# The input projection of layer A, one product at a time over all of k, with 512-column matmuls over both parts of x

## The chip, the cores and the metric

The kernel runs on one core of a Trainium2 chip. The metric is the device time of one execution in microseconds (us); the median of three runs is given, and one further execution was taken with the hardware profiler. TensorE (PE in the profile) multiplies, with PEld for its weight loads; VectorE (DVE), ScalarE (ACT) and GpSimd (POOL) work on tiles in the on-chip memory SBUF, and DVE and ACT also read PE's accumulators in PSUM; SyncE (SP) issues nearly all DMA transfers.

## The reference

Two layers of a small encoder over 512 tokens, width 2048, all in float32. The change is in the first step of layer A, the matrix product `h @ w_in` with its 2048 x 8192 weight:

```python
def pool_mixer_layer(x, norm_g, w_in, w_group, scale, w_out):
    h = rmsnorm(x, norm_g)
    proj = h @ w_in
    u, gate = proj[..., :W_A], proj[..., W_A:]
...
    pooled = jnp.stack(
        [causal_mean_pool(u[:, :, gi], w) - u[:, :, gi] for gi, w in enumerate(POOL_WINDOWS)],
        axis=2)
    y = jnp.einsum('bsgc,gcd->bsgd', pooled, w_group).reshape(B, S, W_A) * scale
    y = y * jax.nn.silu(gate)
    return x + y @ w_out
```

## The kernel before, in words

**Three matmuls for one product.** A float32 product is made of three passes: every operand is split into a rounded high part (dtype fp32r, a copy on ACT) and the rest, the low part (a subtraction on DVE), and PE adds w_hi x_hi, w_hi x_lo and w_lo x_hi in a PSUM accumulator. `split` (L145 to L147) does this for one operand: L146 is the copy on ACT, L147 the subtraction on DVE.

**Seven products for eight.** The projection has 64 blocks of 128 output columns. Four of them (32 to 35) are done in the plain way while x is read in (lines around L372 to L374 of the kernel before). The other 60 are done as 30 pairs. A pair is a 2 x 2 block product: two output blocks by two halves of the tokens (H = 256 tokens each), over the 2048 rows of k, which are taken two tiles of 128 at a time; the eight such steps are called j (NJ = 8). The block product is made with seven products in place of eight, in the manner of Strassen and Winograd: each of the seven multiplies a sum of weight blocks with a sum of x blocks. The seven sums of x are made once (`x_parts`, `x_sums`) and stay in SBUF as `xh[j]` and `xl[j]`, seven slices of 256 columns each. The sums of the weights are made for each pair.

**The loop over pairs (L397 on).** For each pair there are four rounds q of two j. `w_combos` loads the weights of a round (two DMAs of 256 KB, L299, on SP's queue), makes the sums (L302 on DVE, L304 and L305 on POOL), and splits all seven slices at once: L308 on ACT, L309 on DVE, 128 x 1792 each. `seven` then issues, for each of the two j and each of the seven products, the three matmuls L325, L327 and L329, each of 256 columns, 42 in a round and 168 in a pair. The seven products accumulate in seven halves of four PSUM banks (k0 to k3, two sets of them). After the last j `gather` adds the halves into the two outputs (L335 on ACT, L336 to L339 on DVE), and two DMAs (L348) store them in DRAM. For the first eight output blocks `pool_tile` (L241 to L257, on DVE) pools them before they are stored. In the first pairs `square` (L390 to L395) and `norm_r` make the row norms of x beside the loop.

**What sets the order.** Each engine works through its own instructions in the order of the program; a scheduler lays the instructions of all engines out at build time. A tile pool hands out a fixed number of buffers per tag (`bufs`): the write into a reused buffer waits until the last reader of its old content is done. In the loop the tag `raw` has three buffers of 8 KB per partition, `hi` and `lo` two each. SP's queue holds the loads of weights, the stores of outputs and the reads of x, in one order.

**Behind the loop** (L412 on) the stage of the grouped product and the output projection begins: `pooled_tile` reads the first eight pooled blocks back (L424) and `proj` multiplies them with `awg` by three 512-column matmuls for each weight tile (L141 to L143).

## Time and profile before

| what | value |
|---|---|
| median of three runs | 1954.69 us (1954.32 to 1954.99) |
| the profiled execution: its own time | 1954.67 us |
| its span in the profile | 1952.5 us |
| granted TensorE clock, mean over the span | 0.999 |
| PE busy, share of the span | 1920.2 us, 98% |
| DVE, ACT, POOL busy | 1275.8, 820.5, 264.8 us |
| DMA | 235.52 MB, mean 121 GB/s |
| the chain that ended last: PE's share | 91% |

A row of the profile's groups gives line, engine, operation, output and inputs with their shapes, how often, then busy time, mean ns of one, and the idle time of the engine just before with what ended it. A row of the timeline gives the start in us from the span's start, the duration in us, engine, line, operation, how many are merged, and in brackets the idle time before it and what released it. A row of the windows gives a stretch, its length, the busy time of each engine with the number of its instructions, then the granted clock, the busy share of the DMA engines and GB/s. Matmuls overlap in PE's pipeline, so that a matmul's duration is longer than the distance to the next; what PE can do in a time is read from the distances.

### The profile page before, as it was taken

The numbers are of one execution on the slowest core, as the hardware profiler recorded it, in microseconds if no ns is written. First come the engines' busy times: TensorE is split into PE (matmuls) and PEld (weight loads), VectorE is DVE, ScalarE is ACT, GpSimd is POOL, SyncE is SP. The second block draws the span as 40 slices with busy tenths as digits, with TensorE's granted clock in tenths as the row PEclk, the third lists the DMA queues.
The fourth block names the chain that finished last, engine by engine and source line by source line (L and its number), as shares of the span: only waits on it lengthen the run. The fifth ranks groups of instructions, "written<-read, shape, count | busy, mean of one in ns | idle before, by whom it ended". The sixth has DMA issues, their size and how long they took to land.

```text
span 1952.5 us, 30593 instructions
## 1 busy us (share of the span) xinstructions
PE 1920.2 (98%) x11356; PEld 1708.7 (88%) x11356; DVE 1275.8 (65%) x2289; ACT 820.5 (42%) x1561; POOL 264.8 (14%) x404
## 2 busy tenths in 40 slices
PE   8999999999999999999999999999999999999999
PEld 7899999999999878888888888888888888888887
DVE  8766676797666587486695567473344788797432
ACT  7533333333333443333333454332244777785221
POOL 0442323344322100000000000000010111110000
PEclk9999999999999999999999999999999999999999
DMA  6644344335444465334344343333322111121632
GB/s 199 202 135 140 119 138 133 125 125 173 136 124 131 154 212 159 113 121 143 114 130 130 119 146 124 92 92 97 98 92 76 56 39 53 45 70 48 218 119 87
DMA packets 168133, 235.52 MB, mean 121 GB/s; under 512 B 14896, under 2 KB 95152, under 8 KB 167984
## 3 DMA queue, kind: packets, MB, share of 16 engines
q1 hardware_dynamic: 167696, 233.37, 38.0%
q8 instruction: 89, 1.46, 0.3%
q14 instruction: 60, 0.49, 0.1%
q10 hardware_dynamic: 288, 0.20, 0.0%
HBM read 208.35 MB, written 25.17 MB: 120 GB/s over the span
## 4 chain that ended last, share of the span: by engine, by line
PE 91%; DVE 4%; ACT 2%; DMA 1%; issue 1%; SPq 0%; DVEq 0%; ACTq 0%
PE mm L143 16%; PE mm L141 16%; PE mm L142 16%; PE k L329 9%; PE k L325 9%; PE k L327 9%; PE sc L731 2%; PE mm L605 2%; PE mm L607 1%; PE mm L606 1%; PE mm L625 1%; DVE lo L309 1%; PE mm L626 1%; DMA raw<-awin 1%; PE mm L627 1%
## 5 line engine op out<-in xcount | busy, mean ns | idle before, releaser
L123 ACT CAST whi<-raw 128x512 fp32r<-128x512 f32 (+2 forms) x421 | 253.1, 609 | 521.2 <-PE mm L142 451.5
L325 PE MATMUL k<-xh,hi 128*128 128x256 f32 x1680 | 460.0, 283 | 0.0
L327 PE MATMUL k<-xl,hi 128*128 128x256 f32 x1680 | 460.0, 283 | 0.0
L124 DVE TENSOR_TENSOR wlo<-raw,whi 128x512 fp32r<-128x512 f32 (+2 forms) x421 | 281.4, 672 | 231.0 <-ACT whi L123 228.9
L329 PE MATMUL k<-xh,lo 128*128 128x256 f32 x1680 | 418.1, 284 | 4.3 <-DVE lo L309 4.1
L308 ACT CAST hi<-raw 128x1792 fp32r<-128x1792 f32 x120 | 202.8, 1690 | 373.4 <-PE k L329 264.9
L309 DVE TENSOR_TENSOR lo<-raw,hi 128x1792 fp32r<-128x1792 f32 x120 | 248.5, 2071 | 155.7 <-ACT hi L308 155.4
L143 PE MATMUL mm<-bt,wlo 128*128 128x512 f32 x860 | 335.3, 390 | 0.2 <-DVE wlo L124 0.2
L141 PE MATMUL mm<-bt,whi 128*128 128x512 f32 x860 | 334.8, 389 | 0.0
L142 PE MATMUL mm<-bt,whi 128*128 128x512 f32 x860 | 334.5, 389 | 0.0
L327 PEld LDWEIGHTS k<-xl,hi 128*128 128x128 f32 x1680 | 322.5, 192 | 0.0
L325 PEld LDWEIGHTS k<-xh,hi 128*128 128x128 f32 x1680 | 322.5, 192 | 0.0
L329 PEld LDWEIGHTS k<-xh,lo 128*128 128x128 f32 x1680 | 296.7, 192 | 6.0 <-DVE lo L309 5.5
L141 PE MATMUL mm<-at,whi 128*128 128x512 f32 x516 | 201.2, 391 | 3.3 <-ACT whi L123 3.3
L143 PE MATMUL mm<-at,wlo 128*128 128x512 f32 x516 | 202.1, 392 | 1.7 <-DVE wlo L124 1.7
L142 PE MATMUL mm<-at,whi 128*128 128x512 f32 x516 | 202.1, 392 | 0.0
L143 PEld LDWEIGHTS mm<-bt,wlo 128*128 128x128 f32 x860 | 161.4, 188 | 34.6 <-DVE wlo L124 0.6
L141 PEld LDWEIGHTS mm<-bt,whi 128*128 128x128 f32 x860 | 161.4, 188 | 33.7 <-ACT whi L123 0.2
L142 PEld LDWEIGHTS mm<-bt,whi 128*128 128x128 f32 x860 | 161.4, 188 | 33.5
L304 POOL TENSOR_TENSOR raw<-raw 128x256 f32<-128x256 f32 x120 | 102.6, 855 | 430.0 <-DVE raw L302 406.4
L143 PEld LDWEIGHTS mm<-at,wlo 128*128 128x128 f32 x516 | 97.3, 188 | 23.6 <-DVE wlo L124 3.4
L141 PEld LDWEIGHTS mm<-at,whi 128*128 128x128 f32 x516 | 97.1, 188 | 23.6 <-ACT whi L123 3.9
(1174 smaller groups left out, 2584.7 us busy)
## 6 DMA issues: line engine op xcount, KB each, us to landing
raw<-awin SPq DMA_DIRECT2D x240, 256.0 KB, 3.3
raw<-awo SPq DMA_DIRECT2D x128, 256.0 KB, 2.8
raw<-bwin SPq DMA_DIRECT2D x80, 256.0 KB, 2.7
raw<-awg SPq DMA_DIRECT2D x64, 256.0 KB, 2.8
raw<-bwo SPq DMA_DIRECT2D x59, 256.0 KB, 2.8
scr<-e SPq DMA_DIRECT2D x56, 256.0 KB, 2.6
raw<-wkvb SPq DMA_DIRECT2D x32, 256.0 KB, 3.0
raw<-wqb SPq DMA_DIRECT2D x32, 192.0 KB, 2.4
```

The lines of the kernel that those rows point to most:

```text
L123: A.copy(hi[:, :n], raw[:, :n])
L124: V.tensor_tensor(lo[:, :n], raw[:, :n], f(hi[:, :n]), ALU.subtract)
L141: T.matmul(dst, wh, xh, start=first, stop=False)
L142: T.matmul(dst, wh, xl, start=False, stop=False)
L143: T.matmul(dst, wl, xh, start=False, stop=last)
L304: G.tensor_tensor(c[:, :, 6, :], c[:, :, 4, :], c[:, :, 2, :], ALU.add)
L308: A.copy(hi, c[:, :, 1:8, :])
L309: V.tensor_tensor(lo, c[:, :, 1:8, :], f(hi), ALU.subtract)
L325: T.matmul(dst, hi[:, j % 2, wi, :], xh[j][:, xi, :], start=first, stop=False, skip_group_check=True)
L327: T.matmul(dst, hi[:, j % 2, wi, :], xl[j][:, xi, :], start=False, stop=False, skip_group_check=True)
L329: T.matmul(dst, lo[:, j % 2, wi, :], xh[j][:, xi, :], start=False, stop=last, skip_group_check=True)
L605: T.matmul(acc, ch[:, tsl], hi, start=(k == 0), stop=False)
```

## The change

The seven products of a pair are now made one after the other, each over all eight j (`in_pair`, which takes the place of `w_combos`, `banks`, `seven` and `gather`). The numbers p1 to p7 below are the order of the `product` calls.

- The high and low part of x lie side by side (`xx`), so that w_hi x_hi and w_hi x_lo are one matmul of 512 columns (L314) into the two halves of a PSUM bank; w_lo x_hi stays a matmul of 256 columns (L316) into the first half. A product is 8 x 2 matmuls, a pair 112 in place of 168.
- The weights of a pair come as two DMAs of 1 MB (L300, tiles m1 and m2), and a sum or a split covers 128 x 1024 (all j) at a time: two sums on DVE (s1 = a21 + a22 at L325; a21 + a11 at L334), two on POOL (s2 = s1 + a11 at L329; s2 + a12 at L338), seven splits (L146 and L147). `hi` and `lo` have three buffers of one product each; `raw` keeps its three buffers of 1 MB, and a pair holds two of them.
- Three banks per pair. ACT reads banks out between products (L324, L327, L331, L333, L336, L343), as the same bank takes up the next product; DVE adds the pieces (L328, L337, L340, L341, L344, L345). `put` stores the outputs, as before.
- The pool behind `pool_tile` and `square` has three buffers in place of six, and the squares one accumulator in place of two.

```diff
-            h = xcp.tile([P, 7, H], F32R, tag="xh", name="xh")
-            lo = xcp.tile([P, 7, H], F32R, tag="xl", name="xl")
-            xh[j], xl[j] = h, lo
+            xx[j] = xcp.tile([P, 7, 2, H], F32R, tag="xx", name="xx")
+            h, lo = xh[j], xl[j] = xx[j][:, :, 0, :], xx[j][:, :, 1, :]
...
+        def in_pair(pair):
+            m1, m2 = (w7.tile([P, NJ, 2, P], F32, tag="raw", name="raw", bufs=3) for _ in range(2))
+            for m, t in enumerate((m1, m2)):
+                nc.sync.dma_start(t.rearrange("p j k n -> p (j k n)"), awin[2 * pair + m])
+            a11, a12, a21, a22 = m1[:, :, 0, :], m1[:, :, 1, :], m2[:, :, 0, :], m2[:, :, 1, :]
+            s1, s2 = (w7.tile([P, NJ, P], F32, tag=t, name=t, bufs=1) for t in ("s1", "s2"))
+            bx, bb, bc = (ps7.tile([P, 2, H], F32, tag=f"k{i}", name=f"k{i}") for i in range(3))
+            def part(a):
+                hi = w7.tile([P, NJ, P], F32R, tag="hi", name="hi", bufs=3)
+                lo = w7.tile([P, NJ, P], F32R, tag="lo", name="lo", bufs=3)
+                split(a, hi, lo)
+                return hi, lo
+            def product(w, xi, b, first, last):
+                hi, lo = w
+                for j in range(NJ):
+                    T.matmul(b, hi[:, j, :], xx[j][:, xi, :, :], start=first and j == 0, stop=False,
+                             skip_group_check=True)
+                    T.matmul(b[:, 0, :], lo[:, j, :], xh[j][:, xi, :], start=False, stop=last and j == NJ - 1,
+                             skip_group_check=True)
...
+            product(part(a11), 2, bx, True, False)
+            A.copy(p1, bx)
+            V.tensor_tensor(s1, a21, a22, ALU.add)
+            product(part(s1), 4, bc, True, False)
+            A.copy(s5, bc)
+            V.tensor_tensor(p1[:, 0, :], p1[:, 0, :], p1[:, 1, :], ALU.add)
+            G.tensor_tensor(s2, s1, a11, ALU.add)
+            product(part(s2), 5, bb, True, False)
+            A.copy(z[:, 0], bb)
+            product(part(a12), 0, bx, False, True)
+            A.copy(p1[:, 1, :], bx[:, 1, :])
+            V.tensor_tensor(a21, a21, a11, ALU.add)
+            product(part(a21), 3, bb, False, False)
+            A.copy(z[:, 2], bb)
+            V.tensor_tensor(e[:, 0, :], p1[:, 1, :], bx[:, 0, :], ALU.add)
+            G.tensor_tensor(s2, s2, a12, ALU.add)
+            product(part(s2), 1, bc, False, True)
+            V.tensor_tensor(z[:, 0], z[:, 0], bc, ALU.add)
+            V.tensor_tensor(z[:, 2], z[:, 2], s5, ALU.add)
+            product(part(a22), 6, bb, False, True)
+            A.copy(z[:, 1], bb)
+            V.tensor_tensor(e[:, 1:4, :], z[:, :, 0, :], z[:, :, 1, :], ALU.add)
+            V.tensor_tensor(e[:, 1:4, :], e[:, 1:4, :], p1[:, 0:1, :].broadcast_to([P, 3, H]), ALU.add)
...
-        tp[0] = c1.enter_context(tc.tile_pool(name="tpool1", bufs=6, **tile_))
+        tp[0] = c1.enter_context(tc.tile_pool(name="tpool1", bufs=3, **tile_))
```

The order of the instructions on each engine is fixed when the kernel is built. On DVE, in the middle of the loop, one pair took these rows before: four rounds of a split (lo) and of a sum for a round to come (raw), with the four additions of the pair that had just ended in between. A number behind a tile's name tells its buffer's content apart; in brackets stands what the instruction waits for.

```order
L309 TENSOR_TENSOR lo_3268<-raw_3261,hi_3267 128x1792 [waits PE_49,Activation_49]
L302 TENSOR_TENSOR raw_3379<-raw_3379 128x2x256 [waits DMAHW3_49,DMAHW2_49]
L309 TENSOR_TENSOR lo_3320<-raw_3313,hi_3319 128x1792 [waits PE_49,Activation_49]
L302 TENSOR_TENSOR raw_3431<-raw_3431 128x2x256 [waits DMAHW7_49,DMAHW6_49,DVE_49]
L309 TENSOR_TENSOR lo_3386<-raw_3379,hi_3385 128x1792 [waits PE_49,Activation_49]
L302 TENSOR_TENSOR raw_3483<-raw_3483 128x2x256 [waits DMAHW1_49,DMAHW0_49,DVE_49]
L309 TENSOR_TENSOR lo_3438<-raw_3431,hi_3437 128x1792 [waits PE_49,Activation_49]
L302 TENSOR_TENSOR raw_3535<-raw_3535 128x2x256 [waits DMAHW3_49,DMAHW2_49]
L336 TENSOR_TENSOR e_3365<-e_3365,k0_3153 128x512 [waits Activation_49]
```

In the changed kernel DVE has these rows at the end of one pair (raw_3123 and raw_3124 are its m1 and m2) and the start of the next (raw_3312 and raw_3313): lo_3248 and lo_3270 are the low parts of p6 and p7 of the pair, lo_3326, lo_3348 and lo_3371 those of p1, p2 and p3 of the next.

```order
L147 TENSOR_TENSOR lo_3248<-s2_3128,hi_3247 128x1024 [waits PE_49,Activation_49]
L325 TENSOR_TENSOR s1_3316<-raw_3313 128x1024 [waits DMAHW1_49]
L334 TENSOR_TENSOR raw_3313<-raw_3313,raw_3312 128x8x128 [waits DMAHW6_49,DVE_49]
L147 TENSOR_TENSOR lo_3270<-raw_3124,hi_3269 128x1024 [waits PE_49,Activation_49]
L337 TENSOR_TENSOR e_3135<-p1_3134,k0_3129 128x256 [waits DMAHW4_49,DMAHW3_49,Activation_49]
L147 TENSOR_TENSOR lo_3326<-raw_3312,hi_3325 128x1024 [waits PE_49,Activation_49]
L341 TENSOR_TENSOR z_3132<-z_3132,s5_3133 128x512 [waits Activation_49]
L340 TENSOR_TENSOR z_3132<-z_3132,k2_3131 128x512 [waits PE_49]
L147 TENSOR_TENSOR lo_3348<-s1_3316,hi_3347 128x1024 [waits Activation_49]
L147 TENSOR_TENSOR lo_3371<-s2_3317,hi_3370 128x1024 [waits PE_49,Activation_49]
L344 TENSOR_TENSOR e_3135<-z_3132 128x768 [waits DVE_49,Activation_49]
L345 TENSOR_TENSOR e_3135<-e_3135,p1_3134 128x768 [waits DVE_49]
```

The sums of the next pair (L325, L334), which wait for its m2, stand in the queue ahead of the low part of p7 of the pair in hand. On SP's queue a pair had eight loads of 256 KB before, each waiting for the DVE alone that frees its buffer, and two stores.

```order
L299 DMA raw_3261<-awin 128x2x256 [waits DMAHW7_49,DMAHW6_49,DVE_49]
L299 DMA raw_3261<-awin 128x2x256
L299 DMA raw_3313<-awin 128x2x256 [waits DMAHW1_49,DMAHW0_49,DVE_49]
L299 DMA raw_3313<-awin 128x2x256
L299 DMA raw_3379<-awin 128x2x256 [waits DMAHW4_49,DMAHW5_49,DMAHW2_49,DVE_49]
L299 DMA raw_3379<-awin 128x2x256 [waits DMAHW3_49]
L348 DMA scr_3149<-e_3143 256x1x256 [waits DVE_49,Activation_49]
L348 DMA scr_3151<-e_3143 128x512
```

In the changed kernel a pair has two loads of 1 MB; m2 (raw_3313 here) goes into the buffer of m1 of the pair in hand (raw_3123) and so waits for DVE and POOL, the last readers of that m1.

```order
L300 DMA raw_3312<-awin 128x2048 [waits DMAHW1_49,DVE_49]
L358 DMA scr_3119<-e_2962 128x512 [waits DMAHW7_49,DVE_49]
L358 DMA scr_3121<-e_2962 128x512 [waits DMAHW0_49]
L300 DMA raw_3313<-awin 128x2048 [waits DMAHW2_49,DVE_49,Pool_49]
L300 DMA raw_3501<-awin 128x2048 [waits DMAHW5_49,DVE_49]
```

The load of m2 for the next pair moved behind the store of the pair that has ended and behind POOL's second sum of the pair in hand.

More of the change, by code (lines that the diff above doesn't have):

```diff
@@ L312, in banks @@
-        def banks():
-            return [ps7.tile([P, 2, H], F32, tag=f"k{i}", name=f"k{i}") for i in range(4)]
-        SEVEN = ((2, 0, 0, 0), (0, 6, 1, 0), (1, 2, 2, 0), (3, 4, 3, 0),
-                 (5, 5, 0, 1), (6, 1, 1, 1), (4, 3, 2, 1))
-        def seven(ks, w, j):
-            hi, lo = w
-            for wi, xi, b, h in SEVEN:
-                dst = ks[b][:, h, :]
-                first, last = j == 0 and h == 0, j == NJ - 1
-                T.matmul(dst, hi[:, j % 2, wi, :], xh[j][:, xi, :], start=first, stop=False,
-                         skip_group_check=True)
-                T.matmul(dst, hi[:, j % 2, wi, :], xl[j][:, xi, :], start=False, stop=False,
-                         skip_group_check=True)
-                T.matmul(dst, lo[:, j % 2, wi, :], xh[j][:, xi, :], start=False, stop=last,
-                         skip_group_check=True)
@@ L341, in gather, with put @@
+        def put(e, pair):
+            for i in range(2):
+                v = e[:, 2 * i:2 * i + 2, :]
                 o = 2 * pair + i
```

59 lines of the change are left out of this document (17 added, 42 removed).

## The prediction

> **What bounds the kernel now.** I read the page first: busy time and the chain that ended last.
>
> ```profile
> PE 1920.2 (98%) x11356; PEld 1708.7 (88%) x11356; DVE 1275.8 (65%) x2289; ACT 820.5 (42%) x1561; POOL 264.8 (14%) x404
> ...
> PE 91%; DVE 4%; ACT 2%; DMA 1%; issue 1%; SPq 0%; DVEq 0%; ACTq 0%
> ```
>
> PE is the bound over the whole span. Next the timeline of PE: first the distances between matmuls in the loop over pairs (340), in a later stage (1400) and in the stretch that mixes both widths (17 to 19), then the two ends of the loop.
>
> ```profile
> 17.73 0.28 PE L372 MATMUL k<-h,hi 128*128 128x256 f32 x1
> ...
> 18.09 0.39 PE L372 MATMUL k<-xh,hi 128*128 128x512 f32 x1
> ...
> 18.78 0.28 PE L373 MATMUL k<-xl,hi 128*128 128x256 f32 x1
> ...
> 55.05 0.28 PE L325 MATMUL k<-xh,hi 128*128 128x256 f32 x1
> ...
> 340.39 0.28 PE L325 MATMUL k<-xh,hi 128*128 128x256 f32 x1
> ...
> 341.11 0.28 PE L325 MATMUL k<-xh,hi 128*128 128x256 f32 x1
> ...
> 666.43 0.28 PE L329 MATMUL k<-xh,lo 128*128 128x256 f32 x1
> 669.25 0.50 PE L141 MATMUL mm<-at,whi 128*128 128x512 f32 x1 [2.54 <-ACT whi L123]
> ...
> 1400.16 0.39 PE L143 MATMUL mm<-bt,wlo 128*128 128x512 f32 x1
> ...
> 1409.68 0.39 PE L143 MATMUL mm<-bt,wlo 128*128 128x512 f32 x1
> ```
>
> From 340.39 to 341.11 lie six matmuls of 256 columns, 0.12 us each. From 1400.16 to 1409.68 lie 42 of 512 columns, 0.227 each. In the mixed stretch three of 256 take 0.36 and three of 512 take 0.69, so mixing costs nothing extra. Two narrow matmuls take 0.240, one wide one 0.227: each matmul carries about 0.013 us beside its columns. A pair is 168 x 0.12 = 20.16 us. The loop lasts from 55.05 to 666.7, 611.6 us: 30 x 20.16 = 604.8 and 6.8 of waits, mostly in its first pairs. In the windows I took one pair's length:
>
> ```profile
> 340.00:360.16 20.16, 20.16 (x170) 20.16 (x169) 12.83 (x12) 7.03 (x6) 5.92 (x9) 1.00 0.43 131
> ...
> 684.00:688.00 4.00, 4.00 (x18) 2.98 (x18) 3.65 (x7) 2.71 (x5) 0.00 (x0) 1.00 1.05 394
> ```
>
> PE is busy throughout, DVE 12.83 us, ACT 7.03, POOL 5.92: nothing else is near its limit. The second row is for the loads: 394 GB/s with the DMA engines full.
>
> **PE's part of the change.** A product of one j is 0.227 + 0.12 = 0.347 in place of 0.36, a pair 7 x 8 x 0.347 = 19.43 us. If PE stayed the bound, 30 x 0.73 = 22 us would go. The question is whether the other engines still deliver a pair in 19.43.
>
> **What DVE, ACT and POOL take for a pair.** Nearest rows, by line (min/median/max ns) and by group:
>
> ```profile
> L293 DVE TENSOR_TENSOR xl<-raw,xh x8: 1220/1222/1760, 11.1 to 46.2; 128x1024 fp32r<-128x1024 f32 x8
> ```
>
> ```profile
> L283 DVE TENSOR_TENSOR xl<-raw,xh x8: 952/954/961, 8.1 to 42.0; 128x768 fp32r<-128x768 f32 x8
> ```
>
> ```profile
> L292 ACT CAST xh<-raw x8: 1028/1042/1055, 10.0 to 45.1; 128x1024 fp32r<-128x1024 f32 x8
> ```
>
> ```profile
> L305 POOL TENSOR_TENSOR raw<-raw x120: 735/742/2508, 46.9 to 651.9; 128x256 f32<-128x256 f32 x120
> ```
>
> ```profile
> L673 POOL TENSOR_TENSOR tt__14055<-xt,qcos x4: 457/460/463, 1442.8 to 1448.9; 128x128 f32<-128x128 f32 x4
> ```
>
> ```profile
> L382 ACT COPY e<-k x4: 575/582/591, 51.1 to 56.7; 128x512 f32<-128x512 f32 x4
> ```
>
> ACT: seven copies of 1024 at 1.04 and five read-outs at 0.58 (one more of 256 columns), about 10.6 us of 19.43: covered. POOL: 0.46 for 128 elements and 0.742 for 256, so 2.2 ns an element; for 1024 I take 2.4 us (estimate from these two; four times the 256 row, 2.97, is the upper end, 2.1 the lower). DVE: seven splits and two sums at 1.22, two additions of 768 at 0.95, two of 512 (0.69, below), two of 256 (about 0.4): 15.1 us, about 14.0 when they stand back to back. By themselves these fit. But DVE and POOL exclude each other, as the timelines of DVE and of POOL show:
>
> ```profile
> 59.80 2.02 DVE L309 TENSOR_TENSOR lo<-raw,hi 128x1792 fp32r<-128x1792 f32 x1
> ...
> 72.61 0.68 DVE L395 TENSOR_TENSOR tt__629<-tt__629,tt__1301 128x512 f32<-128x512 f32 x1
> 73.21 0.69 DVE L302 TENSOR_TENSOR raw<-raw 128x512 f32<-128x512 f32 x1
> ...
> 342.82 0.68 DVE L302 TENSOR_TENSOR raw<-raw 128x512 f32<-128x512 f32 x1
> ...
> 373.66 0.69 DVE L241 SCALAR_TENSOR_TENSOR tt__4038<-e,r 128x512 f32<-128x512 f32 x1
> ...
> 379.44 0.69 DVE L257 SCALAR_TENSOR_TENSOR tt__4044<-tt__4041,tt__4038 128x512 f32<-128x512 f32 x1
> 380.04 1.24 DVE L241 SCALAR_TENSOR_TENSOR tt__4048<-e,r 128x512 f32<-128x512 f32 x1
> 381.38 1.04 DVE L248 TENSOR_TENSOR tt__4051<-tt__4048 128x512 f32<-128x512 f32 x1
> ```
>
> ```profile
> 60.01 2.39 POOL L304 TENSOR_TENSOR raw<-raw 128x256 f32<-128x256 f32 x1 [4.24 <-DMA scr<-e]
> ...
> 343.63 0.74 POOL L304 TENSOR_TENSOR raw<-raw 128x256 f32<-128x256 f32 x1 [3.48 <-DVE raw L302]
> ...
> 379.66 1.07 POOL L304 TENSOR_TENSOR raw<-raw 128x256 f32<-128x256 f32 x1 [3.51 <-DVE raw L302]
> 380.80 1.07 POOL L305 TENSOR_TENSOR raw<-raw 128x256 f32<-128x256 f32 x1
> ```
>
> At 379.66 POOL starts while DVE's L257 runs to 380.1 and needs 1.07 in place of 0.74; DVE's L241, 0.69 alone at 373.66, needs 1.24, as it gets its turn when POOL ends at 380.7; POOL's next waits for L241, DVE's L248 for POOL. At 60.01 POOL starts just behind a long split and ends 0.58 after it (61.82 to 62.40). Whichever starts first runs, the other waits for its end, and they take turns. Before, POOL ran in DVE's idle time (343.63, behind 3.48 us of waiting). The Trainium skill says the same as a rule (SBUF — State Buffer, section "SBUF: two separate sides"): the port pair that the two share is an exclusive lock, which the first holds for its whole instruction, and which a DVE instruction with two SBUF inputs needs. The trace agrees for holds of about 0.6 us; by that rule a POOL sum over 1024 elements holds DVE off for all of its 2.4 us.
>
> With the lock DVE and POOL need 14.0 + 2 x 2.4 = 18.8 us a pair, still below 19.43. So it is the order that decides.
>
> **The loop that closes.** In the changed order DVE has the next pair's s1 and a21 sums ahead of the low part of p7 of the pair in hand. They wait for m2 of the next pair, whose load waits until the m1 of this pair is free: until POOL's second sum and the low part of p4 are done; and POOL's second sum waits for the low part of p3, whose buffer is free when p7 of the pair before has ended. What a load takes:
>
> ```profile
> DMA to landing us min/median/max: 2.7/3.3/5.2
> ```
>
> That is 256 KB; 768 KB more at 394 GB/s are 2.0 us, so 4.7 for 1 MB at least. I take 5.0, since two stores of 256 KB leave just ahead on the same queue; 6.5 is the upper end (another 1.5 if the stores and the other load share its time). From the end of p7 to the end of the next p7, one after the other:
>
> - the last matmul's way through PE 0.28; ACT's copy for p3 1.04; DVE's low part of p3 1.22; DVE's e addition (next in its queue) 0.95; POOL's second sum 2.4; DVE's second e addition, held off meanwhile, 0.95; low part of p4 1.22: together 8.1;
> - m2's load 5.0;
> - s1 1.22 and a21 1.22 on DVE; POOL's s2 sum, which has waited through a21 and takes its turn, 2.4; low part of p7, held off, 1.22; the 15 matmuls of p7 that need it, 8 x 0.12 + 7 x 0.227 = 2.55: together 8.6.
>
> That is 21.7 us (the 0.08 by which instructions back to back overlap, as from 72.61 to 73.21, and the signals between engines of some 0.05 each about cancel). PE needs 19.43, so it waits 2.3 us in each pair, between the first and second matmul of p7. The change adds 1.5 us to a pair of 20.16 where PE's part alone takes 0.7 away.
>
> **The other edits.** `pool_tile` in four pairs adds six DVE operations near 0.69 and two small ones to such a pair, 4.1 us: 18.8 + 4.1 = 22.9, above the loop by 1.2, so 5 us in all; its three buffers for six add waits for stores in the shade of this. Squares and norm put 15 + 12 operations near 0.6, 17 us, on DVE in the first six pairs, whose idle time (21.7 - 18.8 = 2.9 a pair) is 17 us: I take 6 (0 to 12). The start: p1 needs one split where a round needed all seven sums, and three tiles are loaded while the stage ahead still runs; the 6.8 us of waits go. The last pair has no next pair to wait for, -2. Behind the loop the queue of SP now has the last two stores, which wait for the last e, and three weight loads, each waiting for a split, ahead of the read-back of the pooled blocks that the next matmuls need; before, they stood ahead of the last store, and PE waited 2.54 us (669.25). The last e is done 2.8 us after the last matmul, two stores, 3 splits and a load in a queue of 2 MB come after: about 9 us, +6 (3 to 10). More ACT read-outs and the longer loads on SP cost nothing more, being in the 10.6 us above or in the loop.
>
> **The sum.** Loop: 30 x 21.7 + 5 + 6 - 2 = 660 for 611.6, +48; behind it +6. On the profiled execution's 1954.67 (span 1952.5 and 2.2 around it; the median is 1954.69) this makes 2009 us.
>
> **The rivals.**
>
> *PE stays the bound.* If POOL's long sums let DVE through (the trace shows holds of 0.6 us only), the low part of p7 need not wait for POOL, 21.7 - 2.4 = 19.3, and 2.2 more go where e and p4 ran beside POOL: 30 x 19.43 + 5 = 588, +6 behind: 1937 us, faster. For it: all sums fit. Against it: turns taken by the instruction at 379 to 382. It decides at a loop of 19.8. Chance 0.10.
>
> *The loop closes sooner,* with the load at its 4.7, POOL at 2.1 and signals cheaper by 0.3 in all: 20.5 us, 30 x 20.5 + 9 = 624, +6: 1973. Chance 0.12.
>
> *The load comes late and the clock falls.* With 6.5 for the load the loop is 23.2: 705 for 611.6, +6: 2054. PE would then wait 3.8 us in a piece. In windows of one us, and PE's timeline:
>
> ```profile
> 670.00:671.00 1.00, 0.00 (x0) 0.00 (x0) 1.00 (x2) 1.00 (x3) 0.00 (x0) 0.84 0.78 240
> 671.00:672.00 1.00, 0.77 (x2) 0.68 (x3) 1.00 (x3) 1.00 (x3) 0.00 (x0) 0.50 0.91 270
> ...
> 673.00:674.00 1.00, 1.00 (x4) 0.71 (x4) 1.00 (x2) 0.17 (x1) 0.00 (x0) 0.50 1.12 287
> ```
>
> ```profile
> 91.46 0.75 PE L329 MATMUL k<-xh,lo 128*128 128x256 f32 x4 [1.90 <-DVE lo L309]
> ```
>
> After four us with two matmuls the granted clock fell to 0.50, at the gap of 1.90 it stayed at 1.00. A clock halved for some 3 us (671 to 674) costs 1.5 a pair more, up to 2100. The Trainium skill (TensorE: Matmul & The Clock Gate, section "Part 1: The HAM clock gate") puts the fall behind an idle window of about 3.4 us; by that rule the 2.3 us of my forecast leave the clock alone, which both rows bear out, and 3.8 would not. Chance 0.13.
>
> **How the numbers follow.** My forecast, loop 21.1 to 22.3 and so 1991 to 2027, has 0.65; the likeliest is 2009. The range of 8 in 10 leaves out the first rival and the far half of the third: 1965 to 2060. About 0.2% (4 us) is what a measurement of this kernel can tell from no change. Faster takes the first rival and a hundredth of the second, 0.11; within 0.2% 0.02; slower 0.87.
>
> **What would show it.** Right: PE's waits at L316 for DVE's low part (L147), one of about 2.3 us in nearly every pair, pairs 21.7 us apart; DVE idle at L325 for the DMA of raw; POOL's L338 and L329 of about 2.4 us or longer, with DVE's next operation stretched by as much; distances of 0.227 and 0.12 at L314 and L316. Wrong: pairs 19.4 apart, or DVE's operations unstretched beside POOL's, or m2 landed before DVE reaches s1; a wait of PE at L314 for ACT would be another loop than mine.

## The result and the profile after

The changed kernel takes 2013.64 us (median of 4 runs, 2012.32 to 2017.1), the kernel before in the same session 1954.73 (1954.32 to 1954.99): a ratio of 1.0304, 95% interval 1.0286 to 1.0322. It is slower by 58.9 us. The profiled execution of it took 2014.42 us, its span is 2012.6.

The page of the changed kernel, busy time, granted clock and the chain that ended last:

```profile
PE 1927.7 (96%) x9676; PEld 1627.0 (81%) x9676; DVE 1417.7 (70%) x2379; ACT 911.0 (45%) x1801; POOL 262.0 (13%) x224
...
PEclk9989999999999989999999999999999999999999
...
PE 73%; DVE 9%; DMA 4%; issue 3%; ACT 3%; DVEq 0%; SPq 0%; ACTq 0%
```

PE's share of the chain fell from 91% to 73%; DVE, DMA and "issue" (an engine that waits for nothing the profile shows) took the rest. Where PE waits, by the view of the waits of PE (total us, times, longest):

```profile
PE k L316 <- DVE lo L147: 41.7, 30, 3.8
PE mm L141 <- ACT at L146: 10.6, 1, 10.6
PE k L314 <- ACT hi L146: 9.0, 5, 2.6
```

Of the thirty waits for a low part 27 stand in p7, one in each of 27 pairs, the place that the prediction named; the other three, of less than 0.5 us, stand in p4. The second row is the transition behind the loop, the third lies in the first pairs. The stage runs from 55.5 to 720.1 by PE's timeline, 664.6 us where it took 611.6. Behind it the span is 1292.5 us long, where it was 1285.8: 6.7 more. 53.0 and 6.7 make up the loss.

One turn of the loop, in DVE's timeline, from the low part of p3 of one pair to the low part of p7:

```profile
509.39 1.23 DVE L147 TENSOR_TENSOR lo<-s,hi 128x1024 fp32r<-128x1024 f32 x1 [0.16 <-ACT hi L146]
510.54 0.95 DVE L344 TENSOR_TENSOR e<-z 128x768 f32<-128x768 f32 x1
511.52 3.04 DVE L345 TENSOR_TENSOR e<-e,p 128x768 f32<-128x768 f32 x1
514.48 1.21 DVE L147 TENSOR_TENSOR lo<-raw,hi 128x1024 fp32r<-128x1024 f32 x1
...
517.64 1.23 DVE L147 TENSOR_TENSOR lo<-s,hi 128x1024 fp32r<-128x1024 f32 x1 [0.47 <-ACT hi L146]
520.60 1.23 DVE L325 TENSOR_TENSOR s<-raw 128x1024 f32<-128x1024 f32 x1 [1.74 <-DMA raw<-awin]
521.86 1.23 DVE L334 TENSOR_TENSOR raw<-raw 128x1024 f32<-128x1024 f32 x1
523.00 3.42 DVE L147 TENSOR_TENSOR lo<-raw,hi 128x1024 fp32r<-128x1024 f32 x1
```

The same time on POOL (its second sum, then its first), on ACT (the split of p3 of this pair and of the next), on SP's queue (the load of m2) and on PE (the wait in p7):

```profile
510.70 3.05 POOL L338 TENSOR_TENSOR s<-s,raw 128x1024 f32<-128x1024 f32 x1 [6.35 <-DVE lo L147]
521.96 3.38 POOL L329 TENSOR_TENSOR s<-s,raw 128x1024 f32<-128x1024 f32 x1 [8.21 <-DVE s L325]
```

```profile
508.30 1.06 ACT L146 CAST hi<-s 128x1024 fp32r<-128x1024 f32 x1 [4.02 <-PE k L314]
...
529.54 1.05 ACT L146 CAST hi<-s 128x1024 fp32r<-128x1024 f32 x1 [3.56 <-PE k L316]
```

```profile
515.76 0.33 SPq L300 DMA_DIRECT2D raw<-awin  x1
```

```profile
526.48 0.39 PE L316 MATMUL k<-xx,lo 128*128 128x256 f32 x1 [1.05 <-DVE lo L147]
```

Read in order of time: p7 ends and ACT splits p3 (508.30); DVE its low part; POOL's second sum starts beside L344, and L345 needs 3.04 in place of 0.95, since it waits for POOL's end at 513.75; the low part of p4 ends at 515.69 and 0.07 later m2's load is issued; s1 starts at 520.60, when it has landed; POOL's first sum waits through the a21 sum to 523.09, and the low part of p7 behind it needs 3.42 in place of 1.22; at 526.48 PE gets it, and p7 ends at about 529.26 (taken as 0.28, a matmul's duration, before ACT's next split of p3 at 529.54). A turn is 529.54 - 508.30 = 21.24 us.

How general that is, by line on DVE and POOL (min/median/max ns) and on the page's list of loads (KB, median us to landing; the row of L338 with its longest time, 8977 ns, is taken up with the first pairs below):

```profile
its engine sat idle before it (us, times) until:
  DMA raw<-awin: 56.8, 27
```

```profile
L338 POOL TENSOR_TENSOR s<-s,raw x30: 2413/3050/8977, 57.6 to 703.0; 128x1024 f32<-128x1024 f32 x30
```

```profile
raw<-awin SPq DMA_DIRECT2D x60, 1024.0 KB, 4.9
```

The first is DVE ahead of L325: idle for m2 in 27 of 30 pairs, 2.1 us each. The third is the load's landing, forecast at 5.0.

### The profile page after: what moved, and what is told of

It reads as the page before. It is cut to its first block, busy times and chain, and to the rows that moved or that the text cites. A ratio compares the mean times of both kernels' runs of the same rounds, so it can differ in the third digit from the quotient of the medians.

```text
span 2012.6 us, 26861 instructions
## 1 busy us (share of the span) xinstructions
PE 1927.7 (96%) x9676; PEld 1627.0 (81%) x9676; DVE 1417.7 (70%) x2379; ACT 911.0 (45%) x1801; POOL 262.0 (13%) x224
## 4 chain that ended last, share of the span: by engine, by line
PE 73%; DVE 9%; DMA 4%; issue 3%; ACT 3%; DVEq 0%; SPq 0%; ACTq 0%
PE mm L141 16%; PE mm L142 15%; PE mm L143 15%; PE k L314 10%; PE k L316 5%; DVE lo L147 5%; DMA raw<-awin 3%; PE sc L734 1%; PE mm L608 1%; PE mm L609 1%; PE mm L610 1%; DMA raw<-wkvb 1%; PE tr L704 1%; PE tr L753 1%; PE mm L628 1%
## 5 line engine op out<-in xcount | busy, mean ns | idle before, releaser
L314 PE MATMUL k<-xx,hi 128*128 128x512 f32 x1680 | 599.4, 403 | 9.0 <-ACT hi L146 9.0
L316 PE MATMUL k<-xx,lo 128*128 128x256 f32 x1680 | 470.1, 286 | 41.9 <-DVE lo L147 41.7
L314 PEld LDWEIGHTS k<-xx,hi 128*128 128x128 f32 x1680 | 317.6, 191 | 82.2 <-ACT hi L146 10.6
L316 PEld LDWEIGHTS k<-xx,lo 128*128 128x128 f32 x1680 | 323.6, 193 | 60.1 <-DVE lo L147 55.4
L147 DVE TENSOR_TENSOR lo<-raw,hi 128x1024 fp32r<-128x1024 f32 x120 | 205.2, 1710 | 2.4 <-ACT hi L146 2.4
L146 ACT CAST hi<-raw 128x1024 fp32r<-128x1024 f32 x120 | 126.1, 1051 | 146.4 <-PE k L314 144.8
L146 ACT CAST hi<-s 128x1024 fp32r<-128x1024 f32 x90 | 94.5, 1050 | 194.1 <-PE k L314 141.2
L338 POOL TENSOR_TENSOR s<-s,raw 128x1024 f32<-128x1024 f32 x30 | 111.4, 3712 | 189.2 <-DVE lo L147 189.2
L147 DVE TENSOR_TENSOR lo<-s,hi 128x1024 fp32r<-128x1024 f32 x90 | 111.6, 1245 | 31.5 <-ACT hi L146 30.7
L329 POOL TENSOR_TENSOR s<-s,raw 128x1024 f32<-128x1024 f32 x30 | 97.5, 3252 | 268.9 <-issue 158.0
```

What stands on the lines that cost most here:

```text
L146: A.copy(hi, src)
L147: V.tensor_tensor(lo, src, f(hi), ALU.subtract)
L314: T.matmul(b, hi[:, j, :], xx[j][:, xi, :, :], start=first and j == 0, stop=False, skip_group_check=True)
L316: T.matmul(b[:, 0, :], lo[:, j, :], xh[j][:, xi, :], start=False, stop=last and j == NJ - 1, skip_group_check=True)
L329: G.tensor_tensor(s2, s1, a11, ALU.add)
L338: G.tensor_tensor(s2, s2, a12, ALU.add)
```

## The experiments

Each edit is to the changed kernel (2013.6). In what was expected, theory A is the loop of the prediction; its rivals are named there. "Pairs" are the distances between the starts of L325 on DVE, in the change 21.0 to 21.6 in most pairs: from 499.61 to 691.95 lie nine, 21.37 on average.

**Both sums on DVE.** In place of POOL:

```diff
-            G.tensor_tensor(s2, s1, a11, ALU.add)
+            V.tensor_tensor(s2, s1, a11, ALU.add)
...
-            G.tensor_tensor(s2, s2, a12, ALU.add)
+            V.tensor_tensor(s2, s2, a12, ALU.add)
```

> Both sums that POOL forms in a pair (L329, L338) are formed by DVE. Theory A, the loop that closes from p7 to p7 over POOL's second sum, m2's load and the lock: the loop is 0.28 + 1.04 + 1.22 + 0.95 + 1.22 + 0.95 + 1.22 = 6.9, m2's load 5.0, then s1 1.22, low part of p7 1.22 and 2.55 on PE, 16.9 us in all, below PE's 19.43. Pairs 19.4 to 19.6 apart, no stretched operation on DVE, no long s2 sum in the first pairs: stage about 588 for 664.6, time 1937 (1932 to 1950). Rival B, m2's load has a buffer too late whatever DVE and POOL do: DVE still waits about 2 us at L325 in each pair, PE at L316, pairs 20.5 to 21.3, time 1985 to 2010. Rival C, DVE and POOL together are the bound by their shared time: DVE alone needs 14.0 + 2 x 1.14 = 16.3, time 1937 as by A.

Measured: 1937.04 us (1936.34 to 1938.37), ratio to the kernel before 0.9907 (0.9892 to 0.9922). It is faster than both. In windows of its stage (us, PE, PEld, DVE, ACT, POOL, clock, DMA):

```profile
200.00:400.00 200.00, 200.00 (x1149) 175.02 (x1148) 173.29 (x189) 103.25 (x134) 0.33 (x3) 1.00 0.38 135
```

PE is never idle there. The stage is 587.3 us (56.1 to 643.4), 19.58 a pair with its two ends, forecast 588: PE's part of the change is what the prediction said. DVE took on 2.3 us a pair and the kernel became 77 us faster: that speaks against the load's late buffer as the whole cause (rival B), but not yet against the shared time (C).

**A fourth raw buffer, and the room for it alone.** The second edit holds only what makes the room.

```diff
-            m1, m2 = (w7.tile([P, NJ, 2, P], F32, tag="raw", name="raw", bufs=3) for _ in range(2))
+            m1, m2 = (w7.tile([P, NJ, 2, P], F32, tag="raw", name="raw", bufs=4) for _ in range(2))
...
-            s5 = epool.tile([P, 2, H], F32, tag="s5", name="s5", bufs=1)
+            s5 = z[:, 1]
...
-            e = epool.tile([P, 4, H], F32, tag="e", name="e", bufs=2)
+            e = epool.tile([P, 4, H], F32, tag="e", name="e", bufs=1)
```

> A fourth raw buffer, so m2 of the next pair loads without waiting for m1 of this one; POOL keeps its sums. (Room for it: e has one buffer, s5 lies in z[:,1], the first stage's raw weights lie in s1 and s2, the tiles of pool_tile are 12 columns shorter.) Theory A: the load leaves the loop, and what is left runs over DVE and POOL alone: 0.28 + 1.04 + 1.22 + 0.95 + 2.4 + 0.95, four low parts and p1's sum 4.0, s1 and a21 2.44, POOL's sum 2.4, low part of p7 1.22 and 2.55 on PE, 19.5 us and waits for ACT: pairs 20.0 to 20.6, with the slow first pairs (+15) and pool_tile pairs at 22.9 (+10) a stage of about 631, time 1980 (1968 to 1992). Rival B, the load's late buffer alone: pairs at PE's 19.43, time 1940 to 1957. Rival C, the shared time of DVE and POOL: nothing gained, 2005 to 2015, DVE's idle time at L325 only moves.

> The edits that make room for the fourth raw buffer, without it: e with one buffer, s5 in z[:,1], raw weights of the first stage in s1 and s2, shorter tiles in pool_tile. By every theory none of them lies in the loop: 2013 us (2008 to 2018), pairs 21.3 apart as before. If it differs by more, the comparison with four raw buffers goes against this run.

Measured: 1967.94 us (1966.53 to 1970.42), ratio 1.0065 (1.0050 to 1.0080), at the lower end of A's range; the room alone 2006.62 in one run, 5.7 below the lowest of the changed kernel and 1.4 below the range expected for it. What the room alone gained lies behind the stage, where it takes 1286.0 us in place of 1292.5 (see the transition below). The stage itself takes 663.6 us with the room alone, as in the changed kernel (664.6), and 617.3 with the fourth buffer: the buffer gains 46 us there. The whole times differ by 38.7, since the run with four buffers has the long wait behind the stage again (10.26 us). POOL kept its sums and its time on the lock, so the shared time (C) is not the bound of the changed kernel; nor do pairs fall to 19.43 as by B: most are 19.7 to 20.1 apart. In the order that the scheduler made with four buffers, s1 of the next pair stands well behind the low part of p7, so this run opens the loop at two places at once, as DVE's timeline of it shows (the first row is p7's low part):

```profile
564.80 3.15 DVE L147 TENSOR_TENSOR lo<-raw,hi 128x1024 fp32r<-128x1024 f32 x1 [0.41 <-ACT hi L146]
...
572.90 1.23 DVE L325 TENSOR_TENSOR s<-raw 128x1024 f32<-128x1024 f32 x1 [0.56 <-DMA raw<-awin]
```

The next run moves the order alone.

**The order alone.** s1 of the next pair is queued behind the low part of p7 on DVE; issue_after sets the order and adds no wait.

```diff
-            V.tensor_tensor(s1, a21, a22, ALU.add)
+            with tc.issue_after(low7[-1]) if low7 else ExitStack(): V.tensor_tensor(s1, a21, a22, ALU.add)
...
-            product(part(a22), 6, bb, False, True)
+            w = part(a22); low7.append(nc.cur_bb.bb.instructions[-1]); product(w, 6, bb, False, True)
```

> One thing moves on DVE: s1 of the next pair (and the a21 sum with it) stands behind the low part of p7 of the pair in hand, so DVE's wait for m2 has no longer p7's low part queued behind it. The sums stay on POOL, the raw buffers are three. Theory A, it is the order that closes the loop: m2 then lands 13.1 us after the end of p7 and is needed only for p2, so the loop is open; what is left are DVE and POOL with their lock, 19.5 to 20.5 a pair: with the starved sums of the first pairs (+15) and pool_tile pairs (+10) a stage of about 627, time 1976 (1965 to 1988). Rival B, the load's late buffer alone: m2 lands as late as before and what needs it comes as late, at most 1 us a pair gained, 1985 to 2013. Rival C, the shared time of DVE and POOL: nothing gained, 2008 to 2015.

Measured: 1970.92 us (1970.62 to 1971.91), ratio 1.0083 (1.0068 to 1.0098); 42.7 less than the change. DVE's timeline in this run:

```profile
571.98 1.23 DVE L147 TENSOR_TENSOR lo<-raw,hi 128x1024 fp32r<-128x1024 f32 x1 [1.30 <-ACT hi L146]
574.04 1.23 DVE L325 TENSOR_TENSOR s<-raw 128x1024 f32<-128x1024 f32 x1 [0.84 <-DMA raw<-awin]
575.19 0.41 DVE L337 TENSOR_TENSOR e<-p,k 128x256 f32<-128x256 f32 x1
575.52 3.38 DVE L334 TENSOR_TENSOR raw<-raw 128x1024 f32<-128x1024 f32 x1
```

and POOL's:

```profile
575.40 2.41 POOL L329 TENSOR_TENSOR s<-s,raw 128x1024 f32<-128x1024 f32 x1 [9.28 <-ACT hi L146]
```

The low part of p7 is through when DVE comes to wait for m2, and POOL's first sum now holds off the a21 sum, which PE needs much later. Same buffers, same loads, same sums on the same engines, and pairs of 19.6 in place of 21.4. B allowed 1 us a pair at most.

**One sum at a time.** Only the second line of the first edit, and only the first:

> Only POOL's second sum (L338) goes to DVE; the first (L329) stays on POOL. Theory A: m1 is free 2.4 - 1.2 sooner and no DVE operation is held off ahead of it, and in the new order the low part of p7 stands right behind s1, ahead of POOL's turn: the loop falls to 16.9; POOL's first sum still holds DVE off for 2.2 us a pair, now behind the low part of p7, which leaves a chain on DVE of about 20 us. Pairs 19.6 to 20.2, no starved sum in the first pairs: time 1958 (1945 to 1972). Rival B, the load's late buffer alone: m1 comes free sooner by as much, pairs near 19.43, 1937 to 1950. Rival C: DVE 15.1 and POOL 2.4 make 17.5, PE is the bound, 1937.

> Only POOL's first sum (L329) goes to DVE, where it stands between s1 and the a21 sum, all ahead of the low part of p7; the second (L338) stays on POOL. Theory A, the loop over POOL's second sum, m2's load and the sums ahead of the low part of p7: 8.1 up to the load, 5.0 for it, then s1, s2, a21 and the low part of p7 at 1.22 each and 2.55, 20.5 in all. With the starved second sum of the first pairs left (+15) and four pool_tile pairs (+4) the stage is about 634, time 1983 (1970 to 1995). Rival B, the load's late buffer alone: the second sum still holds m1, so nothing is gained, 2005 to 2015. Rival C, the shared time: DVE 15.1 and POOL 2.4 are 17.5, PE is the bound, 1937.

Measured: the second sum on DVE 1950.78 us (1948.36 to 1951.8), ratio 0.9972 (0.9961 to 0.9984); the first 1975.82 (1973.69 to 1977.99), ratio 1.0107 (1.0092 to 1.0122). Rival C, which put both at 1937, is out. For the second sum the time lies 1 us from the end of B's range and 7 below A's middle, so this run alone would not decide between them; for the first B's 2005 is 29 away. Each sum costs, 63 us the second and 38 the first. That the second costs more because it holds m1 is not shown: in its run the scheduler had also put the low part of p7 right behind s1 (512.78 and 513.92 on DVE), while the other run kept the order (s1, s2, a21 sum, low part of p7).

**Both sums on DVE, with the order kept.** In the first experiment the scheduler had also put the low part of p7 right behind s1. Here both sums of the next pair are written ahead of that low part and it is queued behind them:

```diff
-            product(part(a22), 6, bb, False, True)
+            ready = None if nxt is None else head(nxt)
+            with tc.issue_after(nc.cur_bb.bb.instructions[-1]) if ready else ExitStack():
+                w = part(a22)
+            product(w, 6, bb, False, True)
```

(head loads m1 and m2 and forms s1 and the a21 sum.)

> Both sums on DVE, with the low part of p7 held behind s1 and the a21 sum of the next pair, as in the changed kernel (the two sums are written ahead of it, and on DVE it is queued behind them). It keeps the order that closes the loop and takes away only POOL's long turns. Theory A: the loop is 0.28 + 1.04 + 1.22 + 0.95 + 1.22 + 1.22 = 5.9 to the freeing of m1, 5.0 for the load, then s1 1.22, a part of e 0.41, a21 1.22, the low part of p7 1.22 and 2.55, 17.5 in all, below PE's 19.43: time 1938 (1935 to 1946). Rival H, the order alone makes the loop long, and what moved the sums to DVE gained was that the low part of p7 then stood right behind s1: pairs stay at 21 or more, 1985 to 2013.

Measured: 1940.68 us (1939.61 to 1941.33), ratio 0.9919 (0.9902 to 0.9935). Its DVE timeline:

```profile
561.53 1.23 DVE L300 TENSOR_TENSOR s<-raw 128x1024 f32<-128x1024 f32 x1 [1.51 <-DMA raw<-awin]
562.67 0.41 DVE L339 TENSOR_TENSOR e<-p,k 128x256 f32<-128x256 f32 x1
563.00 1.22 DVE L301 TENSOR_TENSOR raw<-raw 128x1024 f32<-128x1024 f32 x1
564.14 1.22 DVE L147 TENSOR_TENSOR lo<-raw,hi 128x1024 fp32r<-128x1024 f32 x1
```

DVE still waits for m2 with the low part of p7 behind it, 1.51 us here, and nothing is lost by that but some 4 us: without POOL's long turns the same loop is shorter than PE's 19.43. Rival H is out. So the order and the turns of POOL, each opened alone, are links of one loop; the load was opened only together with the order, in the run with four buffers. Each opening gives 38 to 77 us, and the gains don't add, because PE's 19.43 stands below.

**The first pairs.** Five pairs in a row, from 68.19 to 194.09, took 125.9 us, 25.2 each, 19 more than five at 21.37. POOL's second sum there, and DVE beside the first of them:

```profile
80.23 8.31 POOL L338 TENSOR_TENSOR s<-s,raw 128x1024 f32<-128x1024 f32 x1 [7.30 <-DVE lo L147]
...
105.79 8.29 POOL L338 TENSOR_TENSOR s<-s,raw 128x1024 f32<-128x1024 f32 x1 [7.91 <-DVE lo L147]
```

```profile
80.07 0.95 DVE L344 TENSOR_TENSOR e<-z 128x768 f32<-128x768 f32 x1
80.94 0.68 DVE L403 TENSOR_TENSOR tt__621<-tt__621,tt__1332 128x512 f32<-128x512 f32 x1
81.54 0.95 DVE L345 TENSOR_TENSOR e<-e,p 128x768 f32<-128x768 f32 x1
...
85.62 0.69 DVE L403 TENSOR_TENSOR tt__621<-tt__621,tt__1513 128x512 f32<-128x512 f32 x1
```

In a plain pair L345 starts 0.03 us after L344 has ended (511.52 against 511.49), as it needs its result; here an addition of squares starts 0.08 before the end, and DVE runs on without a break until 86.31. POOL's sum ends 2.23 later. Two experiments: leave the work out, or move it. The first leaves out the additions and the norm; the second moves them behind L345:

```diff
-            if k:
-                V.tensor_tensor(sq, sq, x, ALU.add)
...
-                ra[0] = norm_r(sq, D, p)
+                ra[0] = rpool.tile([P, S], F32, tag="r", name="r")
+                V.tensor_copy(ra[0], sq)
```

```diff
-            V.tensor_tensor(e[:, 1:4, :], z[:, :, 0, :], z[:, :, 1, :], ALU.add)
+            with tc.issue_after(fill[-1]) if fill else ExitStack(): V.tensor_tensor(e[:, 1:4, :], z[:, :, 0, :], z[:, :, 1, :], ALU.add)
...
-            if n < 8:
+            with tc.issue_after(low[-1]):
+              if n < 8:
```

(low holds the L345 of each pair, fill the last DVE instruction behind it.)

> The 15 additions of squares (L403) and the 12 operations of the norm on DVE are left out of the first pairs (the factor of the norm is a copy of the first square, so the output is not the reference's); the loads of x and ACT's squares stay. Theory A, POOL's second sum is starved there: with work that does not wait for L344 queued behind it, DVE runs on and the sum takes 8.3 to 9.0 us for 3.05, and the first pairs are 25 to 26 us apart for 21.4. Without that work they are 21.4 apart: 19 us less, time 1994 (1988 to 2000). Rival D, the term of the forecast, 27 operations in idle time: 6 us less, 2007 (2002 to 2012). Rival E, the loads of x on the queue of SP delay m2: nothing gained, 2012 to 2015.

> The changed kernel with nothing left out; only the places of the additions of squares and of the norm on DVE move: each pair's stand behind its L345 and ahead of the next pair's L344, so that L345, which needs L344's result, follows L344 at once in every pair with additions. Theory A: POOL's second sum gets its turn in the short gap between L344 and L345 and takes 3.05 us, not 8.3 to 9.0; the additions, 1.2 us of DVE a pair, fit into DVE's idle time at L325; the first pairs fall from 25 to 26 us to 21.4 to 22: time 1995 (1988 to 2002). Rival F: it is the added DVE work that makes these pairs long, wherever it stands, and POOL is starved at another place: 2008 to 2015.

Measured: without the work 1987.87 us (1987.21 to 1989.47), ratio 1.0170 (1.0155 to 1.0185); moved, 2004.14 (1998.96 to 2006.49), ratio 1.0241 (1.0226 to 1.0255). The first gains 25.8, more than the 19 expected (it ends 0.1 below A's range), with the five pairs at 104.3 us, 21.6 less; rivals D and E are out. The second gains half of what was expected, and lies outside the range given for it. POOL's sum in it:

```profile
78.42 3.05 POOL L338 TENSOR_TENSOR s<-s,raw 128x1024 f32<-128x1024 f32 x1 [6.44 <-DVE lo L147]
...
278.58 8.27 POOL L338 TENSOR_TENSOR s<-s,raw 128x1024 f32<-128x1024 f32 x1 [9.04 <-DVE lo L147]
```

Where L345 follows L344 at once, the sum has its 3.05 us back, and the five pairs took 109.9 us, 16 less. The edit brought two new losses: operations of the norm came to stand around L344 in one later pair, where the sum took 8.27 and the pair 27.3, and the additions went to more pairs, some of 22 to 23 us. That the gap behind L344 gives POOL its turn is shown; that the additions themselves cost nothing is not. Nor is all of the gain POOL's turn directly: over the five pairs the mean granted clock was 0.92 in the changed kernel and 1.00 in both experiments, and how much of the 16 and 22 us is the clock, which fell behind PE's longer waits there, the runs don't separate.

**The transition behind the loop.** Three runs on top of both sums on DVE (1937.0): the read-back of the pooled blocks on POOL's queue; besides, ACT's splits of the blocks ahead of those of the later weights; besides, the loads of x later.

```diff
-        nc.sync.dma_start(x, raws[g * 8 + o])
+        (nc.sync if g else nc.gpsimd).dma_start(x, raws[g * 8 + o])
```

```diff
-        A.copy(hi[:, :n], raw[:, :n])
+        with tc.issue_after(gate[3]) if gate and 0 < seen[0] < 6 else ExitStack(): A.copy(hi[:, :n], raw[:, :n])
```

```diff
-                nc.sync.dma_start(x, xT[k])
+                with tc.issue_after(wd[8]): nc.sync.dma_start(x, xT[k])
```

> The kernel with both sums on DVE (1937.0), and besides the read-back of the eight pooled blocks (L427, first group) issued from the queue of POOL, not from SP's, where it stood behind the last two stores and three loads of weights. Theory: PE's 10.4 us of idle time behind the loop is the time of SP's queue; the blocks were stored long before, so they land before the last matmul and PE waits only for ACT's read-out, one split of weights and one of a block, about 2 us, and the clock no longer falls to a half for some 5 us behind it (1 to 2 us more): time 1927.5 (1925 to 1930). Rival: the buffers into which the blocks are read lie where the last pair's tiles lie, so the read-back waits for the end of the pair on any queue, and PE still waits 7 us or more: 1933 to 1937.

> Both sums on DVE, read-back of the pooled blocks on the queue of POOL, and besides ACT's splits of the second to sixth piece of weights stand behind its splits of the first four pooled blocks. Theory: the 10.8 us of PE's idle time behind the loop are ACT's queue, where four splits of weights, the last waiting until 651.28 for its load, stood ahead of blocks that had landed by about 643; now the first block is split right behind the first piece of weights (which landed at 643.5), PE starts 3 to 4 us after the last matmul and waits some 1 to 2 us once more for the second four blocks: about 6 us less than 1937, 1931 (1928 to 1933). Rival: the loads that start together there share the DMA engines, and whichever is split first, the next one is late by as much: 1935 to 1938.

> The kernel with both sums on DVE, the early read-back on the queue of POOL and ACT's splits of the blocks ahead, and besides the sixteen loads of x for the residual (L453, 4 MB) issued behind the ninth load of weights on SP's queue, not right behind the last stores. Theory G: in the run before, PE began 2.9 us after its last matmul and then waited 8.8 us, since those 4 MB filled the DMA engines and the fourth load of weights took 6.4 us and the second four blocks up to 8.5; without them these land in about 3.5 us, PE waits some 1 to 2 us there: 3 + 2 in place of 10.4, time 1931 (1928 to 1934). Rival: the weights, stores and blocks themselves fill the DMA engines, or the loads of x come late for the residual instead: 1936 or more.

Measured: 1937.4 us (1935.85 to 1939.68), 1942.03 (1941.37 to 1942.69) and 1934.88 (1933.98 to 1935.42); ratios 0.9914 (0.9898 to 0.9931), 0.9928 (0.9915 to 0.9942) and 0.9891 (0.9874 to 0.9907). All three missed what the theory gave. The second is 5 us slower than the kernel it was built on. In the first, four of the blocks were read early (issued from 637.88, the last matmul at 641.36) and PE waited 10.8 us all the same, for ACT stood at a split of weights until 651.28. In the second PE started after 2.91 us and then waited again:

```profile
645.72 0.49 PE L141 MATMUL mm<-at,whi 128*128 128x512 f32 x1 [2.91 <-ACT at L146]
...
668.07 0.80 PE L142 MATMUL mm<-at,whi 128*128 128x512 f32 x1 [8.80 <-DVE at L147]
```

In the third the two long waits became 3.53 and 1.46 with two short ones between, 6.0 in all for 10.4, and 2.2 us were gained, with no overlap between the two sets of times: less than the wait lost. The theory of one queue (SP's) as its cause has fallen.

The room-only run shows what the wait hangs on. There the scheduler had put six of the eight read-backs far ahead on SP's own queue (issued from 485.3 to 487.6), and ACT's splits of the first three of these blocks ahead of its splits of the weights (from 719.32). PE's timeline behind its last matmul, which starts at 718.52:

```profile
721.54 0.50 PE L141 MATMUL mm<-at,whi 128*128 128x512 f32 x1 [2.75 <-ACT whi L123]
...
723.11 0.80 PE L141 MATMUL mm<-at,whi 128*128 128x512 f32 x1 [0.72 <-ACT whi L123]
```

These are 3.5 us of waits in place of 10.55, and the span behind the stage is the 1286 us of the kernel before. So the place of the read-backs and of the splits, on both queues, makes the long wait; the early read-back of four blocks alone did not shorten it. It is one run, and no edit was made to set this order.

## Why the prediction was right, and where it was not

**The sum.** Forecast 2009 us, measured 2013.6; +54 against +59. Forecast loop 660 us, measured 664.6; behind it +6, measured +6.7. The mechanism was right; that the sum came so close is in part luck, as the terms below show.

**PE's part** (7 x 8 x 0.347 = 19.43 us a pair): borne out by the run with both sums on DVE, where PE is busy throughout and a pair takes 19.58 with the stage's ends in it.

**The lock.** POOL's sum over 1024 elements was put at 2.4 us; undisturbed it took 2.41. DVE's operation behind it was stretched by 2.1 to 2.2 us (0.95 to 3.04, 1.22 to 3.42). The Trainium skill's rule of an exclusive lock for a whole instruction (SBUF — State Buffer, section "SBUF: two separate sides") holds for these long sums too: the first rival, that they let DVE through, is out. By the same rule a DVE operation needs the lock with two SBUF inputs or in a 2-port mode; L337 reads PSUM and one tile of SBUF, and in the run with the order alone it took 0.41 us (575.19) while POOL's first sum, started at 575.40, was not delayed by it and took 2.41.

**The loop.** Forecast 8.1 + 5.0 + 8.6 = 21.7, measured in the turn shown 7.7 (from p7's end, taken as 0.28 before ACT's split at 508.30, to 515.69), 4.9, and 8.7 (520.60 to 529.26): 21.24, nine pairs at 21.37. The part that was too long is the first: POOL started beside L344, not behind it. That the loop closes over POOL's turns, the load and the order is shown by the runs that open it, the order and POOL's turns each alone, the load not.

**PE's wait** was put at 2.3 us a pair. Most are listed with 1.0 to 1.7 at L316, 41.7 us in all. The view counts from a matmul's end, which lies behind the start of the next in a busy stretch, so a wait costs about 0.3 more than it lists: the one listed as 1.05 made 1.66 us from 525.04 (L314) over 526.48 (L316) to 526.70 (L314), where 0.227 and 0.12 are the distances without it.

**The clock.** The prediction said that gaps of 2.3 us leave the clock alone. That is wrong. PE's waits in two pairs, and windows of one us around a third, where it waited 2.68 us at L316 until 438.46 (the column behind POOL is the granted clock):

```profile
505.48 0.39 PE L316 MATMUL k<-xx,lo 128*128 128x256 f32 x1 [1.73 <-DVE lo L147]
...
612.06 0.39 PE L316 MATMUL k<-xx,lo 128*128 128x256 f32 x1 [1.98 <-DVE lo L147]
```

```profile
436.00:437.00 1.00, 0.00 (x0) 0.00 (x0) 1.00 (x1) 0.31 (x1) 1.00 (x1) 1.00 0.00 0
437.00:438.00 1.00, 0.00 (x0) 0.00 (x0) 1.00 (x1) 0.00 (x0) 0.32 (x1) 1.00 0.00 0
438.00:439.00 1.00, 0.54 (x3) 0.45 (x4) 1.00 (x3) 0.00 (x0) 0.00 (x0) 0.92 0.00 0
439.00:440.00 1.00, 1.00 (x5) 0.90 (x4) 1.00 (x3) 0.00 (x0) 0.00 (x0) 0.50 0.56 106
```

After waits of 1.98, 2.20 and 2.68 us at L316 the clock fell to 0.50 for 3.4 us; after 1.73 and less at L316 it stayed at 1.00. The Trainium skill (TensorE: Matmul & The Clock Gate, section "Part 1: The HAM clock gate") names an idle window of about 3.4 us, longer than these waits; the measurement decides. With four falls in the first pairs the clock was at 0.50 for 30.7 us of the stage. What that cost is not shown; at half the clock it is at most half of it, 15 us (an estimate).

The length of a wait does not decide by itself. In the room-only run a wait of 2.69 us left the clock at 1.00, and one of 1.81 brought it down (PE's timeline, then windows behind the two waits):

```profile
436.55 0.39 PE L316 MATMUL k<-xx,lo 128*128 128x256 f32 x1 [2.69 <-DVE lo L147]
...
632.15 0.39 PE L316 MATMUL k<-xx,lo 128*128 128x256 f32 x1 [1.81 <-DVE lo L147]
```

```profile
436.00:440.00 4.00, 3.45 (x19) 2.98 (x20) 4.00 (x7) 0.63 (x1) 0.00 (x0) 1.00 0.56 207
...
633.50:636.50 3.00, 3.00 (x12) 2.61 (x11) 2.39 (x4) 0.34 (x1) 0.00 (x0) 0.50 0.78 317
```

In every trace of this case the stretches at 0.50 begin whole multiples of 3.413 us apart; those at 264.76, 438.84 and 612.92 of the changed kernel lie 51 such steps from each other. Counted back from the fall at 633.26, a step of the room-only run ends at 435.29, in the middle of the wait of 2.69, while the wait of 1.81 lies within one step. The wait of 1.90 in the kernel before, which the prediction showed with the clock at 1.00, lies across such an end too (90.41, counted back from the fall at 670.68). That the idle time within one step is what counts is read from this, not tested. How much of it is enough stays open: the room-only run's wait of 2.81 until 115.36 had 1.88 of it in one step, and the clock stayed.

**The first pairs** are the term that was mis-sized: +6 (0 to 12) for squares and norm, measured +19. The step took their 17 us on DVE as covered by 17 us of idle time. Their own time was covered; what they cost was POOL's turn, 4 to 6 us of it in each of four pairs, s2, its product and the freeing of m1 behind it, and a share of unknown size by the clock, which was at 0.50 for 20.5 us of these pairs. The loop of the plain pairs came out shorter by 0.33, 8 us over the other 24, so the two errors hid each other in part.

**pool_tile** pairs: +5 forecast; from 409.77 to 499.61 lie four, 89.8 us, 4.4 more than four at 21.37.

**The transition**: forecast a gap of about 9 us, measured 10.55 (730.65). The size was right. Its cause, SP's queue alone, was not: with the read-back on another queue the wait was as long, and it was 3.5 us in the room-only run, where six blocks were read long before and ACT split the first of them ahead of the weights.

**The second and third rival.** A load of 4.7 and a loop of 20.5 did not come; nor did a load of 6.5, but the falling clock of the third rival was there, in seven places of the stage.

## What to carry over

When work is moved to make one engine's instructions longer and fewer, follow one buffer from its release to the next time that its release is needed, through every queue it passes; if that turn is longer than the bound engine's share, the turn is the new bound, and busy times that all fit don't show it. A long GpSimd operation between VectorE operations with two SBUF inputs cost its whole length on both here, so two sums of 1.2 us a pair on VectorE were cheaper here than two of 2.4 on GpSimd, by 73 us over thirty pairs with the order of the queue kept. Where an in-order queue waits for a transfer, look at what stands behind the wait: moving that one instruction ahead of it gave back 43 us.

## What was not expected of the hardware

POOL and DVE do not simply take turns. POOL's second sum got the port behind L344 in every pair in which L345, which needs L344's result, came next, and was passed over by five to nine operations in a row in the four pairs of the changed kernel in which another stood there. Its first sum got its turn at a boundary without a gap (502.01, with the a21 sum until 502.09). In the run with four buffers the second sum did so too, ahead of a low part at 577.31 that was stretched to 3.43. What decides between these is open.

The granted clock fell after idle times of PE from 1.81 us, where 3.8 us had been taken as the danger, and stayed at 1.00 after others of up to 2.81; where a wait lies among steps of 3.413 us seems to matter more than its length.
